# A gated MLP's down projection as seven half-size products, run in three blocks between the up tiles

## The chip, the core and the metric

The kernel runs on one core of a Trainium2 chip. The metric is the device time of one execution in microseconds (us). Five engines matter: TensorE (PE in the profile) does matmuls and transposes into PSUM, VectorE (DVE) and ScalarE (ACT) do elementwise work, GpSimd (POOL) does a few small powers, and SyncE (SP) issues the DMAs. Each engine works through its own list of instructions in order; semaphores hold an instruction until what it needs is done. A scheduling layer orders each list before the run and hands out the buffers of each pool.

## What is computed

The program is two encoder layers on 512 tokens of width 1024. The change touches the second half of each layer:

```
def conv_glu_ffn(x, w_up, conv_w, conv_b, w_down):       # x: 512 x 1024
    h = x @ w_up                                          # 512 x 5632
    hp = jnp.pad(h, ((0, 0), (1, 1), (0, 0)))
    h = hp[:, :-2] * conv_w[0] + hp[:, 1:-1] * conv_w[1] + hp[:, 2:] * conv_w[2] + conv_b
    a, b = jnp.split(h, 2, axis=-1)                       # 512 x 2816 each
    return (jax.nn.gelu(a) * b) @ w_down                  # 2816 x 1024
...
        ffn = conv_glu_ffn(x, w_up[i], conv_w[i], conv_b[i], w_down[i])
        ple = jax.nn.sigmoid(x @ w_ple_gate[i]) * (p[i] @ w_ple_proj[i])
        x = layer_norm(DEEPNORM_ALPHA * x + ffn + ple, ln2_g[i], ln2_b[i])
```

## The kernel before, in words

**Numbers in two parts.** Every matmul operand is split into a high part `hi` (ScalarE casts it, L96) and a rest `lo` (VectorE subtracts, L97). A product of two operands is three matmuls, `mm3` (L148 to L151): hi times hi, hi times lo, lo times hi, summed in PSUM. So each unit of matmul work comes as three instructions of 128x128 weights by 512 columns.

**Weights as a stream.** `Stream` (L99) brings all weights in the order of use, in 148 chunks of 128x1024 floats (512 KB) for each layer. `load` issues the DMA on SP into one of `N_RAW` = 3 raw buffers (L115); `prep` splits a chunk into one of `N_W` = 3 pairs of buffers in pool `wsplit`; `get` prepares two chunks ahead of the one handed out. Chunks listed in `RESIDENT` (L33) take their pair from pool `unit` instead (`up` in the code, 27 buffers of 4 KB in each partition), so that more of them can be ready. The last four of a layer are among these.

**The up projection.** For each of 22 tiles of 128 hidden channels (L677), two calls of `gemm_t` (L153; 24 matmuls each) give the two halves with channels on partitions and tokens on columns. ScalarE scales the middle tap (L683), VectorE adds the two neighbours (L684, L685), ScalarE applies gelu (L687), VectorE multiplies (L688), and the product is split (L690) into a buffer `gt` that stays until the down projection. All 22 pairs come first.

**The down projection.** It is one call of `proj_ln` (L217, called in L707) with 11 chunks for each of two column halves. For a chunk, `gn_part` (L163) does four token tiles with two blocks of 128 hidden channels each. This is 22 x 4 x 2 x 3 = 528 matmuls in a layer. The sums of a half stay in four PSUM banks for all 11 chunks. `half` then adds them to the residual tile `R` and takes the statistics (L224). In the second column half the last four chunks are worked token tile by token tile (`gemm_n_tok`, L181): so the layer norm of one tile (L235 to L239, with a power on GpSimd in L199) runs beside the matmuls of the next, and `done` of the tile before it is called. In the first layer, `done2` stores the tile to a scratch tensor and transposes it for the next layer (`to_xt`, L202); in the last it stores to the output. The transposes of the fourth tile wait in `pending` and run inside the next layer's first matmuls (L590).

Of the kernel before, what the change touches and what calls it, by code (L numbers as in the profile page):

```python
# [40 lines left out]
def _f(a):  # L41
    return a.bitcast(F32)


def trunk(tc, wpack, x_nat, x_tr, p_tr, rpb, decay, ln_par, conv, cos_t, sin_t, dist, xi_d, zd, mask, ident_d, out):
# [3 lines left out]
    with ExitStack() as es:  # L49
# [18 lines left out]
        def unit_r(s):  # L68
            return up.tile([P, 2, 512], F32R, tag="u", name=nm(s))
# [10 lines left out]
        def small(s, n):  # L80
            return sp.tile([P, n], F32, tag=f"s{n}", name=nm(s))
# [10 lines left out]
        nc.gpsimd.memset(mhalf, -0.5)  # L92


        def split(hi, lo, src):
            nc.scalar.copy(hi, src)  # L96
            nc.vector.tensor_sub(lo, src, _f(hi))  # L97

        class Stream:  # L99


            def __init__(self):
                self.seq = [(l, c) for l in range(DEPTH) for c in range(NCH)]
                self.nload = self.nprep = self.nget = 0
                self.raw, self.rdy = {}, {}

            def load(self, n, part=None):

                while self.nload < min(n, len(self.seq)):
                    l, c = self.seq[self.nload]  # L110
                    if self.nload not in self.raw:
                        self.raw[self.nload] = rp.tile([P, 1024], F32, tag="raw", name=f"raw_{l}_{c}")
                    r = self.raw[self.nload]
                    cs = slice(0, 1024) if part is None else slice(part * 512, (part + 1) * 512)
                    nc.sync.dma_start(r[:, cs], wpack[l, c][:, cs])  # L115
                    self.nload += part != 0
                    if part == 0:
                        return

            def prep(self, n, part=None):  # L120
                while self.nprep < min(n, len(self.seq)):
                    if part is None:
                        self.load(self.nprep + 1)
                    l, c = self.seq[self.nprep]
                    r = self.raw[self.nprep]
                    if self.nprep not in self.rdy:
                        pl, th, tl = (up, "u", "u") if (l, c) in RESIDENT else (wp, "hi", "lo")
                        hi = pl.tile([P, 1024], F32R, tag=th, name=f"hi_{l}_{c}")
                        lo = pl.tile([P, 1024], F32R, tag=tl, name=f"lo_{l}_{c}")
                        self.rdy[self.nprep] = (hi, lo)  # L130
                    hi, lo = self.rdy[self.nprep]
                    cs = slice(0, 1024) if part is None else slice(part * 512, (part + 1) * 512)
                    split(hi[:, cs], lo[:, cs], r[:, cs])
                    if part == 0:
                        return
                    del self.raw[self.nprep]
                    self.nprep += 1

            def get(self, ahead=2):
                self.prep(self.nget + 1 + ahead)  # L140
                self.load(self.nprep + N_RAW)
                w = self.rdy.pop(self.nget)
                self.nget += 1
                return w

        ws = Stream()

        def mm3(ps, lh, ll, rh, rl, start, stop):  # L148
            nc.tensor.matmul(ps, lh, rh, start=start, stop=False)  # L149
            nc.tensor.matmul(ps, lh, rl, start=False, stop=False)  # L150
            nc.tensor.matmul(ps, ll, rh, start=False, stop=stop)  # L151

        def gemm_t(xs, nk=8, wt=None, off=0):  # L153

# [15 lines left out]
        def gemm_n(lh, nchunk, pss, upto=None, post=None, ahead=lambda c: 2):  # L170
# [24 lines left out]
        def rstd_of(var, eps, n):  # L195
            v = small("ve", n)
            nc.vector.tensor_scalar_add(v, var, eps)
            r = small("rstd", n)
            nc.gpsimd.tensor_tensor(r, v, mhalf[:, :n], ALU.pow)  # L199
            return r  # L200
# [9 lines left out]
        def ln_consts(l, which):  # L210
# [3 lines left out]
            nc.sync.dma_start(b, ln_par[l, 2 * which + 1:2 * which + 2, :].to_broadcast([P, D]))  # L214
            return g, b

        def proj_ln(lh, nchunk, z, add, g, b, done, follow):  # L217

            st = [sp.tile([P, 2, 6], F32, tag="bn", name=nm("bn")) for _ in range(4)]

            def half(t, cb, ps):
                zz = z[t][:, cb * 512:(cb + 1) * 512]
                add(zz, ps)
                nc.vector.bn_stats(st[t][:, cb, :], zz)  # L224


            n1 = nchunk - 4
            deep = 4 + follow
            drain(gemm_n(lh, nchunk, [], post=lambda t, ps: half(t, 0, ps), ahead=lambda c: max(2, deep - 2 * (nchunk + n1 - 1 - c))))
            pss = []  # L230
            drain(gemm_n(lh, nchunk, pss, upto=n1, ahead=lambda c: max(2, deep - 2 * (n1 - 1 - c))))
            for t in gemm_n_tok(lh, nchunk, pss, nchunk - 4):
                half(t, 1, pss[t])
                mv = small("mv", 2)
                nc.vector.bn_aggr(mv, st[t])  # L235
                r = rstd_of(mv[:, 1:2], LN_EPS, 1)
                nc.vector.scalar_tensor_tensor(z[t], z[t], mv[:, 0:1], g, op0=ALU.subtract, op1=ALU.mult)
                for c in (slice(0, 512), slice(512, 1024)) if t == 3 else (slice(0, 1024),):
                    nc.vector.scalar_tensor_tensor(z[t][:, c], z[t][:, c], r, b[:, c], op0=ALU.mult, op1=ALU.add)  # L239
                if t:  # L240
                    done(t - 1)

# [57 lines left out]
        for l in range(DEPTH):  # L300
# [281 lines left out]
            if l == 0:  # L582
                drain(gemm_n(lhx, 4, [], post=lambda t, ps: v_tile(0, t, ps)))
                decay_logs()
            else:
                pss = []
                for t in gemm_n_tok(lhx, 4, pss, 0):
                    v_tile(0, t, pss[t])
                    if t == 1:
                        pending()  # L590
            drain(ret_inputs(0, True))

            plan = {}
# [79 lines left out]

            cw = bp.tile([P, 2 * NF, 4], F32, tag="cw", name=nm("cw"))
            nc.sync.dma_start(cw, conv[l])
            gt = []
            for i in range(NF):  # L677
# [11 lines left out]
                u = unit_r("gt")  # L689
                split(u[:, 0, :], u[:, 1, :], half[0])  # L690
                gt.append(u)


            g2, b2 = ln_consts(l, 1)
            last = l == DEPTH - 1
            if not last:
                xt = xp.tile([P, 8, 2, 512], F32R, tag="xt", name=nm("xt"))

            def done2(t, R=R, last=last, xt=xt):
                if last:  # L700
                    for c in (slice(0, 512), slice(512, 1024)):
                        nc.sync.dma_start(out[t * P:(t + 1) * P, c], R[t][:, c])
                else:
                    nc.sync.dma_start(scr[t * P:(t + 1) * P, :], R[t])
                    to_xt(xt, R[t], t)

            proj_ln(lambda k, s, t: gt[k][:, s, t * P:(t + 1) * P], 11, R, lambda zz, ps: nc.vector.tensor_add(zz, zz, ps), g2, b2, done2, 0 if last else 5)  # L707
            pending = lambda: done2(3)
        pending()


def _stat(w):
# [5 lines left out]
def _mov(w):  # L718

    K, N = w.shape  # L720
    return w.reshape(K // 256, 2, P, N // 512, 512).transpose(3, 0, 2, 1, 4).reshape(N // 512, K // 256, P, 1024)


def _pack(w_in, w_ba, w_bb, w_out, w_up, w_down, w_pg, w_pp):
# [20 lines left out]
    su = _stat(w_up)  # L745
    for i in range(NF):
        ch += [su[i], su[NF + i]]
    ch += list(_mov(w_down).reshape(-1, P, 1024))
    assert len(ch) == NCH
    return np.stack(ch)  # L750

# [64 lines left out]
```

## Time and profile before

| | us |
|---|---|
| median of 3 runs (1753.92 to 1754.45) | 1754.08 |
| the profiled execution | 1753.67 |
| its span from first to last instruction | 1751.4 |
| PE busy in the span | 1741.3 |
| VectorE busy | 1041.6 |
| ScalarE busy | 741.5 |
| up stage of the second layer, first to last matmul | 1384.2 to 1623.4 |
| down stage of the second layer, first to last matmul | 1623.6 to 1743.1 |

Two times of an instruction must be kept apart. A matmul's own duration is 389 ns in the rows, but the next one starts before it has ended; the distance from start to start is what a matmul costs the stream. "Busy" is the union of such times for PE. For the other engines durations don't overlap, and a duration is a cost. The idle time in a row is that of the engine just before the instruction, with what ended it.

### The profile page before, as it was taken

How to read it: one execution, taken by the hardware profiler on the slowest of the kernel's cores; microseconds unless marked ns; L12 is line 12 of the kernel's file. 1: busy time of each engine (PE TensorE's matmuls, PEld its weight loads, DVE VectorE, ACT ScalarE, POOL GpSimd, SP SyncE). 2: the span in 40 equal slices, each digit the busy share in tenths (PEclk: the TensorE clock that was granted, in tenths of full speed). 3: DMA queues.
4: the chain of work that ended last, by engine and by line, in shares of the span. 5: the costliest groups of instructions: out<-in, count | busy, mean ns of one | idle time of the engine just before them, and what ended most of it. 6: DMA issues, size and time to landing. Idle time of an engine off the chain costs nothing.

```text
span 1751.4 us, 20526 instructions
## 1 busy us (share of the span) xinstructions
PE 1741.3 (99%) x8169; PEld 1457.2 (83%) x8169; DVE 1041.6 (59%) x1577; ACT 741.5 (42%) x1100; POOL 35.1 (2%) x37
## 2 busy tenths in 40 slices
PE   9999999999999999999999999999999999999998
PEld 7888888888888888888888888888888888888886
DVE  6758766537546666633637687655475566666334
ACT  4535565544234444422234456655332344444220
POOL 0000000000100000000000000000001000000001
PEclk9999999999999999999999999999999999999999
DMA  6222222235122222233422121222351222222331
GB/s 236 87 73 84 69 85 92 89 136 181 48 97 96 97 96 97 96 109 109 162 76 87 61 97 61 95 86 85 133 180 49 93 100 96 97 96 97 108 121 60
DMA packets 52079, 175.78 MB, mean 100 GB/s; under 512 B 6032, under 2 KB 8592, under 8 KB 51984
## 3 DMA queue, kind: packets, MB, share of 16 engines
q1 hardware_dynamic: 51984, 174.48, 29.0%
q8 instruction: 64, 1.05, 0.2%
q14 instruction: 31, 0.25, 0.0%
HBM read 170.26 MB, written 4.19 MB: 100 GB/s over the span
## 4 chain that ended last, share of the span: by engine, by line
PE 96%; DVE 3%; DMA 0%; ACT 0%; issue 0%; POOLq 0%; SPq 0%; DVEq 0%; ACTq 0%
PE gt L150 17%; PE gt L149 17%; PE gt L151 17%; PE gn L150 12%; PE gn L151 12%; PE gn L149 12%; PE na L553 1%; PE pt L541 1%; PE o L151 1%; PE o L150 1%; PE o L149 1%; PE tr L206 1%; DVE lo L97 0%; PE ns L517 0%; PE ns L516 0%; PE ybt L436 0%
## 5 line engine op out<-in xcount | busy, mean ns | idle before, releaser
L97 DVE TENSOR_TENSOR lo<-raw,hi 128x1024 fp32r<-128x1024 f32 (+1 forms) x297 | 361.6, 1220 | 485.0 <-ACT hi L96 480.3
L96 ACT CAST hi<-raw 128x1024 fp32r<-128x1024 f32 (+1 forms) x297 | 310.6, 1049 | 491.8 <-PE gn L151 232.6
L149 PE MATMUL gt<-x1t,hi 128*128 128x512 f32 x704 | 273.9, 389 | 0.0
L150 PE MATMUL gt<-x1t,hi 128*128 128x512 f32 x704 | 273.9, 389 | 0.0
L151 PE MATMUL gt<-x1t,lo 128*128 128x512 f32 x704 | 273.9, 389 | 0.0
L149 PE MATMUL gt<-xt,hi 128*128 128x512 f32 x512 | 200.9, 392 | 0.0
L151 PE MATMUL gt<-xt,lo 128*128 128x512 f32 x512 | 199.6, 390 | 0.0
L150 PE MATMUL gt<-xt,hi 128*128 128x512 f32 x512 | 199.5, 390 | 0.0
L149 PEld LDWEIGHTS gt<-x1t,hi 128*128 128x128 f32 x704 | 132.2, 188 | 27.6
L151 PEld LDWEIGHTS gt<-x1t,lo 128*128 128x128 f32 x704 | 132.2, 188 | 27.3
L150 PEld LDWEIGHTS gt<-x1t,hi 128*128 128x128 f32 x704 | 132.2, 188 | 27.3
L149 PE MATMUL gn<-hi,gt 128*128 128x512 f32 x352 | 137.1, 389 | 0.0
L151 PE MATMUL gn<-hi,gt 128*128 128x512 f32 x352 | 136.9, 389 | 0.0
L150 PE MATMUL gn<-lo,gt 128*128 128x512 f32 x352 | 136.9, 389 | 0.0
L151 PEld LDWEIGHTS gt<-xt,lo 128*128 128x128 f32 x512 | 96.1, 188 | 20.3
L149 PEld LDWEIGHTS gt<-xt,hi 128*128 128x128 f32 x512 | 96.2, 188 | 19.1
L150 PEld LDWEIGHTS gt<-xt,hi 128*128 128x128 f32 x512 | 96.2, 188 | 19.0
L149 PE MATMUL gn<-hi,xt 128*128 128x512 f32 x256 | 100.3, 394 | 0.6 <-ACT hi L96 0.6
L150 PE MATMUL gn<-lo,xt 128*128 128x512 f32 x256 | 99.8, 390 | 0.0
L151 PE MATMUL gn<-hi,xt 128*128 128x512 f32 x256 | 99.7, 389 | 0.0
L96 ACT CAST gt<-ca 128x512 fp32r<-128x512 f32 x44 | 27.3, 621 | 122.0 <-DVE ca L688 122.0
L151 PEld LDWEIGHTS gn<-hi,gt 128*128 128x128 f32 x352 | 66.1, 188 | 13.8
(213 smaller groups left out, 2822.0 us busy)
## 6 DMA issues: line engine op xcount, KB each, us to landing
raw<-in_wpack SPq DMA_DIRECT2D x295, 512.0 KB, 3.2
xst<-in_x_tr SPq DMA_DIRECT2D x8, 256.0 KB, 6.2
xn<-in_x_nat SPq DMA_DIRECT2D x4, 512.0 KB, 6.2
lng<-in_ln_par SPq DMA_DIRECT2D x4, 512.0 KB, 5.0
lnb<-in_ln_par SPq DMA_DIRECT2D x4, 512.0 KB, 5.5
x_scr<-R SPq DMA_DIRECT2D x4, 512.0 KB, 2.6
xn<-x_scr SPq DMA_DIRECT2D x4, 512.0 KB, 6.5
out<-R SPq DMA_DIRECT2D x8, 256.0 KB, 2.0
```

The lines of the kernel that those rows point to most:

```text
L96: nc.scalar.copy(hi, src)
L97: nc.vector.tensor_sub(lo, src, _f(hi))
L149: nc.tensor.matmul(ps, lh, rh, start=start, stop=False)
L150: nc.tensor.matmul(ps, lh, rl, start=False, stop=False)
L151: nc.tensor.matmul(ps, ll, rh, start=False, stop=stop)
L206: nc.tensor.transpose(ps[:, k * P:(k + 1) * P], z[:, (4 * h + k) * P:(4 * h + k + 1) * P], ident)
L541: nc.tensor.transpose(ps[:, i * P:(i + 1) * P], S[:, g * 256 + bb * P:g * 256 + (bb + 1) * P], ident)
L553: nc.tensor.matmul(ov[kt], lv, pt[kt // 2][:, sp_, c], start=i == 0 and sp_ == 0, stop=i == 3 and sp_ == 1)
```

## The change

It does three things. The 22 up tiles of a layer are cut into three groups of 6, 8 and 8 (`SEGS` = 3, 4, 4 pairs), and after each group the part of the down projection that belongs to it is done, with the result added to `R`. That part is no longer eight block products but seven: tokens, hidden channels and output columns are each halved, and with sums and differences of blocks seven products of half size in each dimension are enough (the scheme of Strassen, in Winograd's form). In a pair of up tiles, `g1` and `g2` are the two halves of the hidden channels. Four sums of their token halves are made by VectorE in `s_parts` and split like any operand. The four quadrants of the weights are a, b, c and d. Their sums are not made on an engine: after a raw chunk has been split, a DMA issued by GpSimd adds the next quadrant to the chunk in place (`accum_op`), and the sum is split in turn. One chain goes a, a+b, a+b+d, a+b+c+d; another sum is b+d.

For `n` pairs a product is 2 x n x 3 matmuls. A product works in PSUM banks `u`, `v` (two each), or `w`, which sums its product over all three groups. After most products VectorE adds or subtracts the banks into `R` (`into`). The chunks of c take their pairs from pool `unit`; a raw chunk of a, and of b+d, is held there too. After the last group, the layer norms of the four tiles run beside the last two products and behind them. `done2` of tiles 0 and 1 is called after the last product, of tiles 2 and 3 in the next layer (or at the end).

```diff
-RESIDENT = {(1, c) for c in range(2)} | {(l, c) for l in range(DEPTH) for b in (68, 144) for c in range(b, b + 4)}
+SEGS = (3, 4, 4)
+LOOK = 3
+HELD = ("c",)
+DEEP = 4
+RESIDENT = {(1, c) for c in range(2)} | {(l, c) for l in range(DEPTH) for c in range(68, 72)}
...
+        def down_items(l, s):
...
+            for kind, src, plus in (("a", "a", None), ("c", "c", None), ("t1", None, "b"), ("t2", None, "d"),
+                                    ("d", "d", None), ("t3", "b", "d"), ("t4", None, "c")):
+                for j in range(2):
...
+                    it = Item(kind, at(src), pos["a", j][3], plus=at(plus), own=kind in ("a", "t3"), pool=up if kind in HELD else None)
+                    if kind in ("a", "t1", "t2", "t4"):
+                        if j in prev:
+                            prev[j].nxt = it
+                        prev[j] = it
...
+            def add(self, it):
+                l, c, o, w = it.plus
+                nc.gpsimd.dma_start(it.raw[:, :w], wpack[l, c][:, o:o + w], accum_op=ALU.add)
...
+                    if it.nxt is not None:
+                        it.nxt.raw = it.raw
+                        self.add(it.nxt)
...
+                def s_parts(p, g1, g2):
...
+                    nc.vector.tensor_sub(ta[:, H1], g2[:, H2], g1[:, H2])
+                    nc.vector.scalar_tensor_tensor(tb[:, H1], ta[:, H1], -1.0, g1[:, H1], **op)
+                    nc.vector.tensor_sub(tb[:, H2], g1[:, H1], g1[:, H2])
+                    nc.vector.scalar_tensor_tensor(ta[:, H2], tb[:, H1], -1.0, g2[:, H1], **op)
+                    sa[p], sb[p] = unit_r("sa"), unit_r("sb")
+                    split(sa[p][:, 0, :], sa[p][:, 1, :], ta)
+                    split(sb[p][:, 0, :], sb[p][:, 1, :], tb)
...
+                    split(a11[p][:, 0, :], a11[p][:, 1, :], g1[:, H1])
...
+                    split(k2[p][:, 0, :], k2[p][:, 1, :], g2)
...
+                def product(kind, ps, first):
...
+                    if kind == "t4":
+                        w = [ws.get(1), ws.get(2)]
+                        order = [(j, kk, i) for i in range(2) for j in range(2) for kk in range(2)]
+                    else:
+                        order = [(j, kk, i) for j in range(2) for i in range(2) for kk in range(2)]
...
+                        mm3(ps[i], lh(p, 0, i), lh(p, 1, i), hi[:, r], lo[:, r], first and p == 0, p == n - 1, not first)
...
+                product("a", u, True)
+                s_parts(*sums.pop())
+                for i in range(2):
+                    into(i, N1, u[i])
+                product("c", w, s == 0)
+                if fin:
+                    for i in range(2):
+                        into(i, N1, w[i])
+                        stats(i, 0)
+                product("t1", v, True)
+                for i in range(2):
+                    into(2 + i, N2, v[i], ALU.subtract)
+                product("t2", u, False)
+                for i in range(2):
+                    into(i, N2, u[i], ALU.subtract)
+                product("d", v, False)
+                for i in range(2):
+                    into(i, N2, v[i], ALU.subtract)
+                    stats(i, 1)
+                product("t3", u, False)
+                if fin:
+                    ln_tile(R[0], st[0], g2c, b2c, 1)
+                for i in range(2):
+                    into(2 + i, N2, u[i], ALU.subtract)
+                if fin:
+                    ln_tile(R[1], st[1], g2c, b2c, 1)
+                for i in range(2):
+                    stats(2 + i, 1)
+                product("t4", u, False)
+                if fin:
+                    done2(0)
+                    done2(1)
+                for i in range(2):
+                    into(2 + i, N1, u[i])
+                    stats(2 + i, 0)
+                    if fin:
+                        ln_tile(R[2 + i], st[2 + i], g2c, b2c, 2)
```

`ln_tile` is the layer norm of L235 to L239 as a function of its own; `fin` is true for the third group. In the built program, the lists of the stages before the up projection are the same as before but for a few places at the start of the second layer.

More of the change, by code (lines that the diff above doesn't have):

```diff
@@ L99, in trunk @@
         class Stream:
             def __init__(self):
-                self.seq = [(l, c) for l in range(DEPTH) for c in range(NCH)]
+                self.seq = []
+                for l in range(DEPTH):
+                    tile = 0
+                    plain = lambda c: self.seq.append(Item("w", (l, c, 0, 1024), 1024, pool=up if (l, c) in RESIDENT else None))
+                    for c in range(UP0):
+                        plain(c)
+                    for s, n in enumerate(SEGS):
+                        for c in range(UP0 + 2 * tile, UP0 + 2 * (tile + 2 * n)):
+                            plain(c)
+                        tile += 2 * n
+                        self.seq += down_items(l, s)
@@ L104, in __init__ @@
                 self.nload = self.nprep = self.nget = 0
-                self.raw, self.rdy = {}, {}
+            def add(self, it):
+                l, c, o, w = it.plus
+                nc.gpsimd.dma_start(it.raw[:, :w], wpack[l, c][:, o:o + w], accum_op=ALU.add)
             def load(self, n, part=None):
                 while self.nload < min(n, len(self.seq)):
[L110 to L115, printed above, removed]
+                    it = self.seq[self.nload]
+                    if it.src is None:
+                        self.nload += 1
+                        continue
+                    l, c, o, w = it.src
+                    if it.raw is None:
+                        if it.own:
+                            it.raw = up.tile([P, 1024], F32, tag="u", name=nm("raw" + it.kind))
+                        else:
+                            it.raw = rp.tile([P, 1024], F32, tag="raw", name=nm("raw"))
+                    cs = slice(0, w) if part is None else slice(part * 512, (part + 1) * 512)
+                    nc.sync.dma_start(it.raw[:, cs], wpack[l, c][:, o + cs.start:o + cs.stop])
+                    if it.plus is not None:
+                        self.add(it)
@@ L123, in prep @@
                         self.load(self.nprep + 1)
[L124 to L130, printed above, removed]
@@ L131, in prep @@
-                    hi, lo = self.rdy[self.nprep]
-                    cs = slice(0, 1024) if part is None else slice(part * 512, (part + 1) * 512)
-                    split(hi[:, cs], lo[:, cs], r[:, cs])
+                    it = self.seq[self.nprep]
+                    if it.hl is None:
+                        pl, th, tl = (up, "u", "u") if it.pool is not None else (wp, "hi", "lo")
+                        it.hl = (pl.tile([P, 1024], F32R, tag=th, name=nm("hi")), pl.tile([P, 1024], F32R, tag=tl, name=nm("lo")))
@@ L134, in prep, with get @@
+                    hi, lo = it.hl
+                    cs = slice(0, it.width) if part is None else slice(part * 512, (part + 1) * 512)
+                    split(hi[:, cs], lo[:, cs], it.raw[:, cs])
                     if part == 0:
                         return
-                    del self.raw[self.nprep]
+                    if it.nxt is not None:
+                        it.nxt.raw = it.raw
+                        self.add(it.nxt)
+                    it.raw = None
                     self.nprep += 1
[L139 to L142, printed above, removed]
+            def get(self, ahead=None):
+                if ahead is None:
+                    n, room = self.nget + 1, N_W - (self.seq[self.nget].pool is None)
+                    while n < min(len(self.seq), self.nget + 1 + DEEP):
+                        it = self.seq[n]
+                        if it.pool is None:
+                            if room == 0:
+                                break
+                            room -= 1
+                        elif it.kind == "w":
+                            break
+                        n += 1
+                    self.prep(n)
+                else:
+                    self.prep(self.nget + 1 + ahead)
+                self.load(self.nprep + LOOK)
+                it = self.seq[self.nget]
+                w, it.hl = it.hl, None
@@ L146, in trunk, with mm3 @@
         ws = Stream()
[L148 to L151, printed above, removed]
+        def mm3(ps, lh, ll, rh, rl, start, stop, more=False):
+            nc.tensor.matmul(ps, lh, rh, start=start, stop=False, skip_group_check=more)
+            nc.tensor.matmul(ps, lh, rl, start=False, stop=False, skip_group_check=more)
+            nc.tensor.matmul(ps, ll, rh, start=False, stop=stop, skip_group_check=more)
         def gemm_t(xs, nk=8, wt=None, off=0):
@@ L168, in gn_part, with gemm_n @@
                 mm3(ps, lh(k, 0, t), lh(k, 1, t), hi[:, r], lo[:, r], k == 0, k == 2 * nchunk - 1)
-        def gemm_n(lh, nchunk, pss, upto=None, post=None, ahead=lambda c: 2):
+        def gemm_n(lh, nchunk, pss, upto=None, post=None, ahead=lambda c: None):
             pss += [bank("gn") for _ in range(4)]
@@ L215, in ln_consts, with ln_tile @@
             return g, b
+        def ln_tile(z, st, g, b, parts):
+            mv = small("mv", 2)
+            nc.vector.bn_aggr(mv, st)
+            r = rstd_of(mv[:, 1:2], LN_EPS, 1)
+            nc.vector.scalar_tensor_tensor(z, z, mv[:, 0:1], g, op0=ALU.subtract, op1=ALU.mult)
+            for i in range(parts):
+                c = slice(i * D // parts, (i + 1) * D // parts)
+                nc.vector.scalar_tensor_tensor(z[:, c], z[:, c], r, b[:, c], op0=ALU.mult, op1=ALU.add)
         def proj_ln(lh, nchunk, z, add, g, b, done, follow):
@@ L233, in proj_ln @@
                 half(t, 1, pss[t])
[L234 to L239, printed above, removed]
+                ln_tile(z[t], st[t], g, b, 2 if t == 3 else 1)
                 if t:
@@ L675, in trunk, with up_tile @@
             nc.sync.dma_start(cw, conv[l])
-            gt = []
-            for i in range(NF):
+            last = l == DEPTH - 1
+            def up_tile(i):
                 half = []
@@ L688, in trunk @@
                 nc.vector.tensor_mul(half[0], half[0], half[1])
[L689 to L705, printed above, removed]
@@ L712, in _stat @@
+            pending = done2
+            if last:
+                pending(2)
+                pending(3)
 def _stat(w):
@@ L721, in _mov, with _blocks @@
     return w.reshape(K // 256, 2, P, N // 512, 512).transpose(3, 0, 2, 1, 4).reshape(N // 512, K // 256, P, 1024)
+def _blocks(w):
+    q = w.reshape(NF // 2, 2, P, 2, 512)
+    piece = lambda k, p0, p1: q[p0:p1, "ab".find(k) < 0 and 1 or 0, :, int(k in "bd")].transpose(1, 0, 2).reshape(P, -1)
+    ch, p0 = [], 0
+    for n in SEGS:
+        if n == 4:
+            ch += [piece(k, p0 + 2 * j, p0 + 2 * j + 2) for k in "acbd" for j in range(2)]
+        else:
+            ch += [piece(k, p0, p0 + 2) for k in "acbd"]
+            ch += [np.concatenate([piece(k, p0 + 2, p0 + 3) for k in kk], axis=1) for kk in ("ac", "bd")]
+        p0 += n
+    return ch
 def _pack(w_in, w_ba, w_bb, w_out, w_up, w_down, w_pg, w_pp):
@@ L747, in _pack @@
         ch += [su[i], su[NF + i]]
-    ch += list(_mov(w_down).reshape(-1, P, 1024))
+    ch += _blocks(w_down)
     assert len(ch) == NCH
```

95 lines of the change are left out of this document (88 added, 7 removed).

## The prediction

> **What bounds the kernel now.** I read the page's shares first, then the list of those who waited, then the groups of the down stage, then the timeline.
>
> ```profile
> PE 1741.3 (99%) x8169; PEld 1457.2 (83%) x8169; DVE 1041.6 (59%) x1577; ACT 741.5 (42%) x1100; POOL 35.1 (2%) x37
> ...
> PE gn L149 <- ACT hi L96: 0.6, 1, 0.6
> ...
> L149 PE MATMUL gt<-x1t,hi x352: 389/389/389, 513.9 to 752.6; 128*128 128x512 f32 x176
> ...
> 513.00:753.00 240.00, 240.00 (x1060) 198.79 (x1059) 146.74 (x177) 104.38 (x133) 0.00 (x0) 1.00 0.29 98
> 753.00:875.00 122.00, 122.00 (x550) 101.19 (x549) 52.62 (x60) 29.59 (x31) 4.33 (x3) 1.00 0.36 125
> 1622.00:1744.00 122.00, 121.44 (x536) 100.26 (x534) 45.06 (x51) 22.80 (x23) 4.34 (x3) 1.00 0.28 95
> ```
>
> PE is always busy, and after the start it waited for nobody longer than 0.6 us: its stream is the time. (The windows give PE, PEld, DVE, ACT and POOL busy, then the granted clock and the DMA share: up stage of layer 1, then the two down stages.) A matmul must not be priced by its 389 ns. The third line has 352 starts, three matmuls apart, from 513.9 to 752.6: 238.7/1053 = 0.2267 us a matmul. What keeps PE whole is slack elsewhere: VectorE is busy 61% in the up stage and about 40% in the down stage.
>
> These rows give the prices of the other engines, and the end of the kernel:
>
> ```profile
> L97 DVE TENSOR_TENSOR lo<-raw,hi 128x1024 fp32r<-128x1024 f32 x295 | 360.2, 1223 | 483.6 <-ACT hi L96 478.9 <-PE gn L151 3.9
> L97 DVE TENSOR_TENSOR gt<-ca,gt 128x512 fp32r<-128x512 f32 x44 | 30.5, 693 | 30.2 <-ACT gt L96 30.2
> L707 DVE TENSOR_TENSOR R<-R,gn 128x512 f32<-128x512 f32 x16 | 10.8, 684 | 20.2 <-PE gn L151 19.9
> L224 DVE BATCH_NORM_STATS2 bn<-R 128x6 f32<-128x512 f32 x16 | 10.7, 688 | 0.3
> L96 ACT CAST hi<-raw 128x1024 fp32r<-128x1024 f32 x295 | 309.4, 1051 | 490.2 <-PE gn L151 232.6 <-PE gt L150 125.1 <-issue 106.5
> ...
> 1743.05 0.39 PE L151 MATMUL gn<-hi,gt 128*128 128x512 f32 x1
> ...
> 1744.93 0.21 DVE L235 BATCH_NORM_AGGREGATE mv<-bn 128x2 f32<-128x12 f32 x1
> 1745.17 0.15 DVE L197 TENSOR_SCALAR ve<-mv 128x1 f32<-128x1 f32 x1
> 1745.24 1.28 DVE L237 SCALAR_TENSOR_TENSOR R<-R,mv,lng 128x1024 f32<-128x1024 f32 x1
> 1746.95 1.41 DVE L239 SCALAR_TENSOR_TENSOR R<-R,rstd,lnb 128x512 f32<-128x512 f32 x2 [0.43 <-POOL rstd L199]
> ...
> DMA to landing us min/median/max: 3.0/3.2/7.1
> ```
>
> A chunk's split is 1.05 us of ScalarE, then 1.22 of VectorE; a row of 512 elements is 0.69, one of 256 0.42 (or 0.48, `scalar_tensor_tensor`). VectorE ends 5.1 us after the stream's last step (1743.28 to 1748.36). The last line is a 512 KB raw chunk, from its issue.
>
> **What goes.** A product of n pairs is 2 x n x 3 matmuls, so a layer has 7 x 6 x 11 = 462 for 528. The built order of the changed kernel has 8027 matmuls for 8159; all 132 come from here, same shape. 132 x 0.2267 = **-29.9 us**, if the stream stays whole.
>
> **What VectorE gets.** A pair of up tiles is 96 matmuls, 21.8 us. VectorE had 4 x 1.22 + 8 x 0.75 + 4 x 0.69 = 13.6; a second split of 0.69 now becomes 0.42 + four sums 1.8 + two splits 1.4, together 16.5 (76%). A product block of four pairs is 168 matmuls, 38.1 us: 14 splits and 12 adds are 17.1 + 8.3 = 25.4. Hidden beside PE on the whole, as ScalarE's half of it is. The third block adds two adds, eight statistics and four layer norms (2.9 each): 25.4 + 1.4 + 5.5 + 11.7 = 44.0 against 38.1. That does not fit, so there I follow the built order of VectorE's list.
>
> **Waits inside the blocks.** Product t4 sums onto bank u, so the add that reads u after t3 must come first. VectorE's list has the splits of both t4 chunks ahead of that add, and the second split needs the buffer that t3's first chunk frees. From that moment PE has 12 matmuls left in t3 (2.72 us), the others 1.05 + 1.22 + 0.69 + 0.1 for gaps = 3.1: 0.35 late. With three pairs: 6 matmuls, 1.36, against 0.62 + 0.69 + 0.69 + 0.1 = 2.1: 0.75 late; there also t1's second chunk finds the sums of the last pair 0.5 late (from the last up matmul VectorE has 9.9 us of rows from 1.1 on, PE 10.9). 1.6 a layer, **+3.2**. Behind these adds in the list stand only the next chunks' splits, half a product early.
>
> **The third block.** Between d's end and the add that frees u, VectorE's list is: two adds, two statistics, a split, two aggregates, `ve`, the first layer-norm row, the other split, the second row, the add: 1.38 + 1.38 + 1.22 + 0.42 + 0.15 + 1.28 + 1.22 + 1.28 + 0.69 = 9.0, with 0.03 between rows 9.4. It can't begin early, since t3's second split fills the time until d ends. PE has only t3, 24 x 0.2267 = 5.4: PE stands for 3.9, in both layers **+7.8**. In layer 1 six transposes of tile 0 stand ahead of t4 and wait for the same rows.
>
> **The seam of the layers.** `done2(2)` is now in the next layer: its transposes are fixed in PE's list 19 matmuls into it. From t4's start VectorE has 19 rows up to tile 2's layer norm (an add, `ln_tile(R[1])`, statistics, four splits of transposes, a chunk's split, two more adds, the norm itself): 14.5, with gaps 15.0. PE has t4 5.4, ten transposes (eight took 1.03) 1.3, 19 matmuls 4.3: 11.0. **+3.9**; behind the waiting transposes stands the whole stream. The old kernel had tile 3 alone left here, and no wait.
>
> **The end.** From t4's start VectorE has `ln_tile(R[1])`, adds and statistics, and two layer norms: 14.1 in rows, 14.6 with gaps, less t4's 5.4 = 9.2 after the last matmul, for 5.1 now: **+4.1**. The output DMAs follow as before.
>
> **The adding DMAs.** There is no such row: GpSimd sent none. Let D be the time from an add's being free to go to its landing. It writes the 512 KB that a raw chunk does, so it is no less than 3.2; it also reads the buffer as a second stream, so at most twice the slowest row, 14.2. I take 5: 3.2, and 1.3 for a second stream at the 412 GB/s of the load at the start, and some for sending; DMA engines are only a third busy here. The cover: count from the last four up calls. They end at 21.8; a+b of chunk 0 is split then (its slot), by 24.1, and now the add of d may go. On ScalarE its split stands ahead of those of the last pair's sums `sa`, `sb`, which t1's second chunk needs at 32.6 (three pairs) or 36.0 (four). Going back over 1.05 + 1.22 + 0.69 and gaps, it must land by 30.1 or 32.9: cover 6.0 and 8.8. At D = 5 it costs **nothing**. On POOL's list the adds wait for each other's splits; b+d stands behind a+b+c+d there, with more cover. The weights are read twice over in all (8 quadrants for 4), in stages whose DMA share is 0.3. On SP's list the next up tiles' chunks stand behind b+d's loads, which wait for a `unit` buffer; they are due several products later.
>
> Sum: -29.9 + 3.2 + 7.8 + 3.9 + 4.1 = -10.9. Against the profiled execution's 1753.67 (span 1751.4 and 2.3 around it; 0.4 under the median) that is **1743**.
>
> **A rule against this change.** Three pauses of 3.9 us might cost more than themselves. The trace: PE's last matmul ends at 1743.4, and the windows show clock 1.00 to 1746, then
>
> ```profile
> 1746.00:1747.00 1.00, 0.00 (x0) 0.00 (x0) 0.56 (x2) 0.00 (x0) 0.92 (x1) 0.61 0.00 0
> ...
> 1.19 4.02 PE L248 MATMUL warm<-warm 128*128 128x512 bf16 x9 [1.19 <-DVE dl L282]
> ```
>
> The clock falls some 2.8 us after work stops, and at the start nine matmuls took 4.02, 0.45 each, twice the later pace. So each pause may cost up to 2 us more. The Trainium skill ("TensorE: Matmul & The Clock Gate", Part 1) says the clock halves after an idle window of about 3.4 us, which does not restart with the work; by that only some pauses of 3.9 would hold a whole window, and the sum would be 1743 or little more.
>
> **Rivals.**
> 1. Slow adds. Place: ScalarE's list before `sa`; price by steps at D = 10: three pairs 8.7 (k2 behind a+b 1.3, t1 4.3 more, t3 3.1), four pairs 3.0, third block 5.3: 17 a layer, +34, so **1777**. At D = 8 it is 3.2 + 1.5 a layer, +9.4, still 1752; from about 8.3 on the kernel is slower. For it: raw rows up to 7.1 and a second stream. Against: the median of 3.2. 0.28, and 0.07 for a D near 8.
> 2. VectorE's excess is hidden: rows overlap better than my chain, the third block's waits are some 1 us each. **1727**: 29.9 less 3.2. Against: the list's order is fixed. 0.13.
> 3. The clock falls in all three pauses: +6, **1749**. 0.12.
> 4. The matmuls are not fewer: excluded by the count.
>
> **How the numbers follow.** Forecast 1743 (0.40, some 1738 to 1747). This measurement tells 0.2% (3.5 us) from nothing. Faster: 0.40 + 0.13 + 0.10 of the third = 0.63; same: 0.07 + 0.02 = 0.09; slower: 0.28. From 1727 to 1775 leaves out a little of rival 2 below and half of rival 1 above (D beyond 10), 0.05 and 0.14.
>
> **What would show it.** Matmuls 132 fewer at 0.227 from start to start. Adds landing within 6 us. PE waiting for VectorE's `R` adds (t4) 0.3 to 0.8 in the first two blocks, 3.9 in the third, and 3.9 at tile 2's transposes; VectorE ending 9 us after the last matmul. Wrong if ScalarE's `hi` splits wait on DMAs for microseconds ahead of `sa`, or if the granted clock falls inside the kernel.

## The result, and the profile after

The changed kernel takes 1757.3 us (median; 1754.3 to 1760.23) where the kernel before takes 1753.88 (1753.42 to 1754.45) on the same chip. The ratio is 1.0019, 95% interval 1.0012 to 1.0026: slower by 0.2%, where 1743 was forecast. The profiled execution took 1758.16, its span 1756.4. The 132 matmuls went as counted (8037 records for 8169), so 29.9 us left PE's stream, and some 34 came in.

The page after the change: each engine's busy time, the DMA queues (packets, MB, share of 16 engines), the chain that ended last, and three DMA issues (KB each, median us to landing):

```profile
PE 1724.1 (98%) x8037; PEld 1436.5 (82%) x8037; DVE 1161.8 (66%) x1811; ACT 791.6 (45%) x1184; POOL 77.4 (4%) x85
...
q1 hardware_dynamic: 52560, 174.48, 29.1%
q0 software_dynamic: 6912, 23.07, 7.4%
...
PE 83%; issue 6%; DVE 5%; DMA 4%; ACT 1%; POOL 0%; SPq 0%; POOLq 0%; DVEq 0%; ACTq 0%
...
raw<-in_wpack SPq DMA_DIRECT2D x271, 512.0 KB, 3.3
rawa<-in_wpack POOLq DMA_DIRECT2D x30, 512.0 KB, 5.9
...
rawt<-in_wpack POOLq DMA_DIRECT2D x10, 512.0 KB, 7.9
```

The chain of the kernel before was:

```profile
PE 96%; DVE 3%; DMA 0%; ACT 0%; issue 0%; POOLq 0%; SPq 0%; DVEq 0%; ACTq 0%
```

PE is still busy 98%, but its part of the chain has gone from 96% to 83%, and DMA has 4% of it, where it had none. The two queues give a price. The loads (q1) hold the 16 engines for 0.291 x 1756.4 x 16 / 174.48 = 47 engine-us per MB, the adding DMAs (q0) for 90. A 512 KB load fills all sixteen for 1.54 us, an add for 2.95.

What PE waits for (in total, times, longest), after; before, after the start, the longest was 0.6:

```profile
PE u L233 <- DVE R L844: 7.4, 5, 2.3
PE v L233 <- ACT hi L101: 4.2, 1, 4.2
PE tr L290 <- DVE R L308: 2.8, 2, 1.5
PE u L234 <- DVE lo L103: 1.8, 4, 0.7
```

The first line is t4 waiting for its bank. The second and the fourth are waits for split weights, `hi` of ScalarE and `lo` of VectorE; nothing of the kind was forecast as a cost. By blocks, as PE time beyond 0.2267 us a matmul:

| stretch | layer 1 | layer 2 |
|---|---|---|
| three pairs | 6.7 | 8.6 |
| middle four pairs | 0.6 | 0.65 |
| third block (layer 1: with the seam) | 10.4 | 4.15 |
| behind the last matmul, over the 5.1 of before | | 2.7 |

About 8.5 of this is no wait but a slow clock behind a wait (the last section says when it comes). The largest piece is the third block of layer 1. In the windows (PE, PEld, DVE, ACT, POOL busy, granted clock, DMA share, GB/s) its first four products and then the pause are seen:

```profile
827.00:849.00 22.00, 22.00 (x98) 18.10 (x97) 17.01 (x24) 8.56 (x10) 5.29 (x6) 1.00 0.90 178
849.00:857.00 8.00, 3.80 (x16) 2.57 (x14) 1.59 (x2) 2.66 (x3) 0.00 (x0) 0.84 0.94 247
```

The DMA engines are not a third busy here but nine tenths, though 178 GB/s at a load's 47 engine-us per MB would be 0.52 of them. In the second window all compute engines starve together. ScalarE's and PE's lists of that moment (start, us, instruction, idle before):

```profile
844.02 1.06 ACT L101 CAST hi<-raw 128x1024 fp32r<-128x1024 f32 x1 [1.41 <-PE v L235]
854.34 1.99 ACT L101 CAST hi<-raw 128x1024 fp32r<-128x1024 f32 x2 [9.26 <-DMA raw<-in_wpack]
```

```profile
856.38 0.80 PE L233 MATMUL v<-hi,sa 128*128 128x512 f32 x1 [4.20 <-ACT hi L101]
857.83 0.79 PE L234 MATMUL v<-lo,sa 128*128 128x512 f32 x1 [0.65 <-DVE lo L103]
```

ScalarE stood 9.26 us for a plain load, a chunk of the next layer that took 8.8 us to land (issued at 845.51), and d's second chunk is behind it in the list. So an add need not be late itself; it makes the loads late. In the block of three pairs it is b+d that is late. GpSimd's list and ScalarE's split of it:

```profile
590.57 0.87 POOL L165 DMA_DIRECT2D rawa<-in_wpack  x1 [5.70 <-DVE lo L103]
591.12 1.22 POOL L165 DMA_DIRECT2D rawt<-in_wpack  x1
```

```profile
598.83 1.05 ACT L101 CAST hi<-rawt 128x1024 fp32r<-128x1024 f32 x1 [3.32 <-DMA rawt<-in_wpack]
```

b+d's add (`rawt`) stands behind a+b+c+d's, which stood 5.70 for a split of t2; then it took 7.6 us to land, the second one 11.0.

### The profile page after: what moved, and what is told of

It reads as the page before. It is cut to its first block, busy times and chain, and to the rows that moved or that the text cites. A ratio compares the mean times of both kernels' runs of the same rounds, so it can differ in the third digit from the quotient of the medians.

```text
span 1756.4 us, 20791 instructions
## 1 busy us (share of the span) xinstructions
PE 1724.1 (98%) x8037; PEld 1436.5 (82%) x8037; DVE 1161.8 (66%) x1811; ACT 791.6 (45%) x1184; POOL 77.4 (4%) x85
## 3 DMA queue, kind: packets, MB, share of 16 engines
q1 hardware_dynamic: 52560, 174.48, 29.1%
q0 software_dynamic: 6912, 23.07, 7.4%
## 4 chain that ended last, share of the span: by engine, by line
PE 83%; issue 6%; DVE 5%; DMA 4%; ACT 1%; POOL 0%; SPq 0%; POOLq 0%; DVEq 0%; ACTq 0%
PE gt L233 15%; PE gt L234 15%; PE gt L235 15%; PE gn L235 8%; PE gn L234 8%; PE gn L233 8%; DMA rawa<-in_wpack 2%; DVE lo L103 2%; PE u L233 2%; PE u L234 1%; PE u L235 1%; DMA rawt<-in_wpack 1%; ACT hi L101 1%; PE na L641 1%; PE pt L629 1%
## 5 line engine op out<-in xcount | busy, mean ns | idle before, releaser
L103 DVE TENSOR_TENSOR lo<-raw,hi 128x1024 fp32r<-128x1024 f32 (+1 forms) x277 | 334.7, 1210 | 344.2 <-ACT hi L101 343.4
L101 ACT CAST hi<-raw 128x1024 fp32r<-128x1024 f32 (+1 forms) x277 | 287.2, 1041 | 409.6 <-PE gt L234 118.4
L235 PE MATMUL gt<-x1t,lo 128*128 128x512 f32 x704 | 273.9, 389 | 0.0
L235 PE MATMUL gt<-xt,lo 128*128 128x512 f32 x512 | 199.6, 390 | 0.0
L235 PEld LDWEIGHTS gt<-x1t,lo 128*128 128x128 f32 x704 | 132.2, 188 | 27.5
L235 PEld LDWEIGHTS gt<-xt,lo 128*128 128x128 f32 x512 | 96.1, 188 | 20.3
L235 PE MATMUL gn<-hi,xt 128*128 128x512 f32 x256 | 99.7, 389 | 0.0
L103 DVE TENSOR_TENSOR lo<-rawa,hi 128x1024 fp32r<-128x1024 f32 (+1 forms) x48 | 54.1, 1131 | 42.0 <-ACT hi L101 42.0
L283 POOL TENSOR_TENSOR rstd<-ve,mhalf 128x2 f32<-128x2 f32 (+1 forms) x32 | 34.9, 1090 | 945.1 <-DVE ve L281 945.1
L101 ACT CAST hi<-rawa 128x1024 fp32r<-128x1024 f32 (+1 forms) x48 | 46.8, 979 | 64.1 <-DMA rawa<-in_wpack 34.2
L773 DVE SCALAR_TENSOR_TENSOR ca<-gt,cw,ca 128x511 f32<-128x511 f32 x88 | 65.5, 744 | 5.4 <-ACT ca L772 5.4
L772 ACT ACTIVATE ca<-gt,cw 128x512 f32<-128x512 f32 x88 | 68.2, 775 | 0.0
```

The source lines that it names most:

```text
L235: nc.tensor.matmul(ps, ll, rh, start=False, stop=stop, skip_group_check=more)
```

## The experiments

The theory: the adding DMAs cost twice the engine time of a plain transfer and crowd the DMA engines within the blocks, so splits come late. Its rivals: GpSimd's queue is slow whatever it carries; or it is VectorE's and ScalarE's order, with the adds only bystanders. The runs of before beside these had medians of 1754.01 (first four), 1754.09 (next four) and 1754.06 (last).

**Without the adds.** The chunks are split and used without the quadrant added, so the sums of the weights are not made.

```diff
-                nc.gpsimd.dma_start(it.raw[:, :w], wpack[l, c][:, o:o + w], accum_op=ALU.add)
+                return
```

> The changed kernel with its adding DMAs left out (so the sums of the weights' quadrants are not made; everything else is computed). Crowding theory (an add takes twice the DMA engines' time of a load, and in a block the 16 engines are full, so that sums and the loads beside them land late and PE stands): with no add in the way, PE's waits for splits (some 18 us with the slow clock behind them) go, and what is left is VectorE's rows at the third block, the seam and the end, 10 to 13 us; 1753.9 - 29.9 + 12 = about 1736. List theory (as in the prediction: the waits come from the fixed order and the amount of VectorE's work, not from DMAs): at most 3 us faster than the changed kernel's 1757, about 1754.

1737.05 us, ratio 0.9903 (0.9888 to 0.9918). Of PE's waits that the change brought, two lines are left:

```profile
PE u L233 <- DVE R L844: 4.6, 5, 2.3
PE tr L290 <- DVE R L308: 2.9, 2, 1.6
```

There is no wait for a split inside the blocks. The adds cost 20.3 us, two thirds of the 29.9 that the matmuls gave. Most of the other third is VectorE's order (the two lines above, and the end) with a slow clock behind one of its waits.

By blocks, PE's time beyond 0.2267 us a matmul falls by 5.7 and 7.5 in the blocks of three pairs and by 7.3 in layer 1's third block with the seam: 20.5 in these two profiles, for the 20.3 of the medians. The middle blocks lose no more with the adds than without (0.6), and neither does layer 2's third block (4.2 for 4.1), though each of them holds the same eight adds. A middle block of the changed kernel, with a DMA share of 0.79 (0.66 in 563 to 601 us, a block of three pairs), has PE busy without a break:

```profile
687.00:725.00 38.00, 38.00 (x169) 31.49 (x168) 28.16 (x38) 17.64 (x23) 7.04 (x8) 1.00 0.79 177
```

Its adds land in 5.5 to 10.3 us, as late as elsewhere. So the crowd alone cost nothing here; it cost where the late transfer had too little cover, that is, time between its landing and its use.

**The same DMAs, not adding.** They overwrite the buffer: same queue, same place in it, same bytes, and the sums are not made.

```diff
-                nc.gpsimd.dma_start(it.raw[:, :w], wpack[l, c][:, o:o + w], accum_op=ALU.add)
+                nc.gpsimd.dma_start(it.raw[:, :w], wpack[l, c][:, o:o + w])
```

> The same DMAs on the same queue in the same order, but they overwrite the buffer and don't add (so the products get a single quadrant for each sum). Crowding theory, with the adding as what doubles the engines' time: DMA share in the blocks falls from 1.0 to about 0.75, landings from 5.9 to about 4 us, time about 1742. If GpSimd's queue itself is what is slow, landings stay near 6 and the time near 1757. List theory: 1755 to 1757.

1739.04, ratio 0.9916 (0.9901 to 0.993). Its queue, and the two issues:

```profile
q0 software_dynamic: 6400, 23.07, 3.7%
...
rawa<-in_wpack POOLq DMA_DIRECT2D x30, 512.0 KB, 3.7
...
rawt<-in_wpack POOLq DMA_DIRECT2D x10, 512.0 KB, 4.8
```

The same 23.07 MB take 3.7% for 7.4%, and `rawa` lands in 3.7 for 5.9. So it is neither the queue nor the second reading of the weights, but the adding: 18.3 us of the 20.3.

**The next layer's first chunks not held back.** In the changed kernel they take pairs of their own from `unit`, and so their split stands ahead of d's.

```diff
-RESIDENT = {(1, c) for c in range(2)} | {(l, c) for l in range(DEPTH) for c in range(68, 72)}
+RESIDENT = {(l, c) for l in range(DEPTH) for c in range(68, 72)}
```

> The changed kernel, with the next layer's first two chunks no longer held in the unit pool, so that their splits don't stand ahead of d's on ScalarE in the first layer's third block. If d's second chunk was late only because ScalarE's list waited for a raw chunk of the next layer that landed late: the pause of 4.6 us, the 1.5 behind it and the slow clock's 1.5 go, about 1750. If the pause has another cause, as the list theory has it (VectorE's rows there), 1756 to 1758.

1754.78, ratio 1.0003 (0.9993 to 1.0013): between the two forecasts, 2.5 under the changed kernel, not the gain that the pause in d would have paid. That pause is gone, but in its place PE waits 3.2 before tile 0's transposes, and at the seam one matmul of the next layer 2.7 behind a layer norm. Most of it only moves. So the pause in d needed both: a load made late by the adds, and a place in ScalarE's list ahead of d's chunk.

**b+d ahead of the block.** Its load and its add are sent with a's loads, before the first product; the other adds stay.

```diff
+                    if kind == "a":
+                        firsts[j] = it
+                    if kind == "t3":
+                        firsts[j].early = it
...
+                    if it.early is not None and not it.early.loaded:
+                        e = it.early
...
+                        nc.sync.dma_start(e.raw[:, :w], wpack[l, c][:, o:o + w])
+                        self.add(e)
+                        e.loaded = True
```

> The changed kernel, with the load and the add of b+d issued together with the loads of a, before the block, so that they no longer stand behind a+b+c+d on GpSimd's list and no longer fall in the block's crowd. Crowding theory: the pauses ahead of t3 and t4 in the three-pair block (2.5 + 2.4 us, and the slow clock behind them 1.5 in layer 1 and 3.0 in layer 2) go in both layers, and DMA share in the blocks falls a little; about 1745. List theory: those pauses are VectorE's adds and stay; 1755 to 1757.

1738.78, ratio 0.9915 (0.99 to 0.9929): faster than both kernels, by more than expected. The same stretches of layer 1's third block, counted from its first matmul, and PE's waits:

```profile
822.00:844.00 22.00, 22.00 (x98) 18.21 (x97) 17.42 (x25) 10.04 (x12) 3.50 (x4) 1.00 0.73 139
844.00:852.00 8.00, 8.00 (x37) 6.62 (x36) 8.00 (x11) 3.65 (x5) 0.00 (x0) 1.00 0.70 229
```

```profile
PE u L246 <- DVE R L857: 4.6, 5, 2.3
PE tr L303 <- DVE R L321: 3.5, 2, 2.2
```

The DMA share is 0.73 for 0.90. The next layer's load at that place lands in 3.2 for 8.8, PE is busy without a break, and the waits for splits are gone as in the run without adds, though all the adds are made. What the adds still cost is 1.7 by the medians (1738.78 to 1737.05), with overlapping intervals. The adds' engine time has not fallen with the crowd: their queue takes 7.7% of the span of 1736.6, 93 engine-us per MB for 90.

**Loads sent five items ahead.** This is to tell whether b+d gained from its place in GpSimd's list or from leaving the crowd: it comes ahead of a+b+c+d in the list, but stays in the block. All other loads of the stream may go two items earlier too.

```diff
-LOOK = 3
+LOOK = 5
```

> The changed kernel with its loads sent five items ahead instead of three. That puts b+d's add ahead of a+b+c+d's in GpSimd's list, but still inside the block, with the same bytes in the same 38 us. Theory A, the crowd in the block (the DMA engines' time): the adds take 7 to 12 us still, and the time is 1752 to 1757. Theory B, b+d stood behind a+b+c+d's add, which waits for a split: PE's waits in t3 of the first block go (2.5 and 2.1, with some of the slow clock behind them), 1746 to 1750.

1747.07, ratio 0.9959 (0.9945 to 0.9974), in the range of theory B.

```profile
584.31 0.87 POOL L165 DMA_DIRECT2D rawa<-in_wpack  x1 [1.17 <-DVE lo L103]
585.16 0.92 POOL L165 DMA_DIRECT2D rawt<-in_wpack  x1
```

```profile
PE v L233 <- ACT hi L101: 3.3, 1, 3.3
```

b+d's first add goes 6 us sooner. It lands in 8.4, no faster, but in time; the blocks of three pairs give back 10.5 of their 15.3 us. The pause in d of layer 1 stays (3.3), with a share of 0.86 in the four products before it. So both theories hold, in different blocks: some 10 us (1757.3 to 1747.07) came with the earlier place in the list, and another 8 (1747.07 to 1738.78) with leaving the block. That the 10 are b+d's place alone is argued from the blocks in which they came back; the edit moves other loads too.

**VectorE's and ScalarE's order, with b+d ahead.** Three runs: the seam's edit again; the two adds that free bank u put ahead of tile 0's layer norm; and both.

```diff
                 product("t3", u, False)
-                if fin:
-                    ln_tile(R[0], st[0], g2c, b2c, 1)
                 for i in range(2):
                     into(2 + i, N2, u[i], ALU.subtract)
                 if fin:
+                    ln_tile(R[0], st[0], g2c, b2c, 1)
                     ln_tile(R[1], st[1], g2c, b2c, 1)
```

> This joins two edits: b+d's load and adding DMA ahead of the block (1738.8 alone), and the next layer's first two chunks no longer held back in the pairs' pool (1754.8 alone, no gain on the changed kernel). Theory A, the adding DMAs' crowd made the pause in d at the end of layer 1: with the crowd thinned that pause has gone already, so the second edit brings nothing, 1738 to 1740. Theory B, ScalarE's order (the next layer's split ahead of d's second chunk) has a price of its own: 1735 to 1737, with the seam's waits gone as well.

> Beside b+d going ahead of the block, in the third group the two adds that free bank u stand ahead of tile 0's layer norm in VectorE's list. Theory A, the order: PE's waits before t4 (2.2 and 2.3) shrink to some 0.5 each, and the slow clock behind the last one (1.7) goes: 1733 to 1735. Theory B, the amount of VectorE's work from d's end on: VectorE has no idle time from there to the transposes in layer 1 and to the last row in layer 2, so what PE gains before t4 it waits for at the transposes of tiles 0 to 2 and behind the last matmul: 1738 to 1739, the waits only in other places.

> All three edits: b+d ahead of the block, the next layer's first two chunks not held back, and the adds that free bank u ahead of tile 0's layer norm. If each of the last two has a gain of its own: 1731 to 1734. If both only move VectorE's work: 1737 to 1739.

The seam's edit: 1742.1 (0.9932, 0.9917 to 0.9946), worse than without it, which neither theory had: a matmul early in the next layer now waits 2.7 for a split behind layer-norm rows. The swap: 1738.0 (0.9909, 0.9894 to 0.9924); both: 1738.59 (0.9913, 0.9896 to 0.9929). The swap's null hides two opposite effects:

```profile
PE u L246 <- DVE R L857: 5.5, 6, 2.1
PE gn L247 <- DVE lo L103: 2.1, 1, 2.1
```

In layer 2 the wait before t4 went from 2.3 to 1.1, and no slow clock followed: about 3 us gained up to VectorE's last row. In layer 1 a chunk's split fell behind a norm (second line), with a slow clock behind it: as much lost.

**The swap in layer 2 alone.**

```diff
+                if fin and not last:
+                    ln_tile(R[0], st[0], g2c, b2c, 1)
                 for i in range(2):
                     into(2 + i, N2, u[i], ALU.subtract)
                 if fin:
+                    if last:
+                        ln_tile(R[0], st[0], g2c, b2c, 1)
```

> b+d ahead of the block, and the adds that free bank u ahead of tile 0's layer norm in the second layer alone. In the run with that order in both layers, layer 2's t4 stopped for 1.1 instead of 2.3 without a slow clock behind it, while in layer 1 a chunk's split fell behind a layer norm and cost about 3 at the seam. If these two are independent, layer 2's part stays alone: 1735 to 1736.5. If VectorE's work from d's end sets the end of the kernel whatever its order: 1738 to 1739.

1736.94, ratio 0.99 (0.9883 to 0.9916): the lowest of the versions that compute the whole, though its interval lies over those of b+d ahead (0.99 to 0.9929) and of the swap in both layers, so that this last step is not shown. It is under the 1738 of the second theory and a little over the first one's range, and its layer 2 shows the shorter wait (1.1, no slow clock), with the same 3.1 gained from the block's first matmul to VectorE's last row as in the swap of both layers.

## Why the prediction was wrong

**The step that failed: "At D = 5 it costs nothing".** The adding DMAs were priced at 0 and cost 20.3, by the profiles 13.2 in the blocks of three pairs and 7.3 in layer 1's third. They landed in 5.9 and 7.9 (the medians of `rawa` and `rawt`) and in up to 11.1, for the 5 assumed. Three parts of that step went wrong.
- "DMA engines are only a third busy here" and "in stages whose DMA share is 0.3". That share was the average of the old down stage. The change puts eight adds into a block of four pairs: 8 x 2.95 = 23.6 us of all sixteen engines in 38.1 us, 62% by themselves, and with the loads 0.79 in a middle block and 0.90 in the first four products of layer 1's third. Even without a row for an add, the text's own 1.3 us for a stream, taken twice for each add, gives 8 x 2.6 = 21 of the 38 us. This made the landings late, but where there was cover, as in the middle blocks, late landings cost nothing.
- "b+d stands behind a+b+c+d there, with more cover". In the blocks of three pairs it had less, and the text gave no number for it. The add ahead of it waits for a split in t2 and holds it on GpSimd's list to 591.12; what matters is not only when it is needed but when it may go.
- The price was put on the add alone. The loads on the other queue pay as well. The text looked at them for the next up tiles only ("they are due several products later"); at the end of layer 1 it is a chunk of the next layer, whose split stands ahead of d's in ScalarE's list. That plain 512 KB load took 8.8 us and stopped PE for the longest time of all.

The cover of `sa`, worked out at length, was nearly right: t1 lost 1.1 in one block of three pairs and 0.3 in the other.

**Rival 1, slow adds, is what came.** For D = 8 it had 1752, for D = 10 1777; 1757.3 lies between. But that number is in part luck, since its place was wrong: not ScalarE's list ahead of `sa`, but b+d in t3 and t4, and d.

**The matmuls: -29.9**, right, by count and by pace (24 in 5.44 us wherever nothing waits).

**Waits in the first two blocks: +3.2** forecast. With b+d ahead, t4 waits 0.77 in the blocks of three pairs and 0.38 in the middle ones, for 0.75 and 0.35; t1's 0.5 does not come. 2.3 in all.

**The third block 3.9 twice, the seam 3.9, the end +4.1**: each there, each too large. In the run with b+d ahead they are 2.2 and 2.3, 1.3, and 2.7 (VectorE ends 7.8 after the stream's last step for 5.1). The chain was priced at durations plus 0.03 between rows. In that run it reads, from d's end in layer 2 (left out are the layer norm's rows and the other split):

```profile
1710.08 1.28 DVE L857 TENSOR_TENSOR R<-R,v 128x512 f32<-128x512 f32 x2
1711.28 1.28 DVE L861 BATCH_NORM_STATS2 bn<-R 128x6 f32<-128x512 f32 x2
1712.47 1.21 DVE L103 TENSOR_TENSOR lo<-rawa,hi 128x1024 fp32r<-128x1024 f32 x1
...
1717.43 1.28 DVE L857 TENSOR_TENSOR R<-R,u 128x512 f32<-128x512 f32 x2
```

Two adds of 0.68 take 1.20 from start to start, 0.60 each. The chain to the end of the add that frees u is 1710.08 to 1718.11, 8.0 and not 9.4. The sections ahead of the prediction say that durations of engines other than PE don't overlap; in these rows VectorE's overlap by 0.08, and the chain came out too long mainly by that.

**The sum, mended.** -29.9 + 2.3 + 2.2 + 2.3 + 1.3 + 2.7, and 1.7 of slow clock, is -17.4; b+d ahead measured -15.2. The 2.2 that are left are in small steps of 0.1 to 0.5 around transposes and norms, and were not followed further. Rival 2 (1727, VectorE's excess hidden) is out: without any add the kernel takes 1737.

**Rival 3, the clock**, came as well, but not at its place: in the changed kernel it fell four times, behind t4 in both blocks of three pairs and in layer 2's third, after pauses of 2.4, and within the pause in d. In all it cost about 8.5 us there, and 1.7 with b+d ahead.

## What to carry to other kernels

Price DMA work in the stage where it runs: sum the engine time of the transfers that fall into one block and hold it against that block's length, because a share averaged over a longer stage hides a block that is nearly full. An adding DMA counts double there, and plain loads in the same window become late with it. Then look for the transfer with the least cover: the middle blocks were crowded too and lost nothing. Where several transfers share one issuing queue, send those that wait for no split first, ahead of the crowded block: here that alone turned +0.2% into -0.85%.

## What the runs showed of the hardware

**An adding DMA** takes 90 engine-us per MB, the same transfer on the same queue without adding 45, a load 47. The chunks `rawa` land in 5.9 (median, 512 KB) where the plain ones do in 3.7. In the crowd of the changed kernel an add took up to 11.1, and a plain load on SP's queue up to 12.9. The Trainium skill ("DMA: Bandwidth & Descriptors", Anatomy of one DMA) fits 2.0 us and the bytes at 436 KB per us for a DMA of GpSimd's, an estimate of 3.2 for 512 KB; the plain run agrees roughly (3.7), the adding one does not.

**VectorE's rows overlap.** An instruction that does not read the result of the one before it starts 0.08 us before that one's end; one that reads it starts 0.03 behind that end. Two rows of the kernel before, the statistics reading what the add wrote, show the second kind (0.72 from start to start, duration 0.69):

```profile
1743.48 0.69 DVE L707 TENSOR_TENSOR R<-R,gn 128x512 f32<-128x512 f32 x1 [0.68 <-PE gn L151]
1744.20 0.69 DVE L224 BATCH_NORM_STATS2 bn<-R 128x6 f32<-128x512 f32 x1
```

**The clock falls when PE stands for about half of a window of 3.41 us.** The trace has the times at which the granted clock goes from 1.0 to 0.5 and back. In each run they lie whole multiples of 3.4133 us apart: in the changed kernel it falls at 608.64, 854.40, 1482.45 and 1738.45, which is 0, 72, 256 and 331 such steps. If each run is cut into windows by these steps, then over all eleven profiles 17 windows between the clock's first rise and the last matmul began at full clock and had PE idle for 1.75 us or more, and the clock fell at the end of each. After some 5500 others, with 1.74 or less, it never fell. It then stays at 0.5 for one window or two, and a matmul costs 0.43 for 0.23: 1.5 to 2.9 us at a time behind the three such waits of t4 in the changed kernel.

So one and the same pause can cost more or less. Here is the wait before the last t4 in the changed kernel and in the one without adds; the last row of each is a stretch of 2 us in which the clock falls (the granted clock is the third number from its end):

```profile
1738.07 0.47 PE L233 MATMUL u<-hi,k 128*128 128x512 f32 x1 [2.28 <-DVE R L844]
1738.38 0.56 PE L234 MATMUL u<-lo,k 128*128 128x512 f32 x1
1738.73 0.63 PE L235 MATMUL u<-hi,k 128*128 128x512 f32 x1
1739.16 0.63 PE L233 MATMUL u<-hi,k 128*128 128x512 f32 x1
...
1738.00:1740.00 2.00, 1.93 (x5) 1.56 (x6) 2.00 (x4) 0.00 (x0) 1.27 (x1) 0.61 0.68 262
```

```profile
1717.60 0.47 PE L233 MATMUL u<-hi,k 128*128 128x512 f32 x1 [2.28 <-DVE R L844]
1717.91 0.39 PE L234 MATMUL u<-lo,k 128*128 128x512 f32 x1
1718.13 0.39 PE L235 MATMUL u<-hi,k 128*128 128x512 f32 x1
...
1718.00:1720.00 2.00, 2.00 (x9) 1.61 (x8) 2.00 (x5) 0.00 (x0) 1.45 (x1) 0.76 0.54 208
```

In the first the window ends 0.4 us behind the pause, and the steps are 0.43 almost at once. In the second it ends at 1719.06, 1.5 behind the pause: the steps are 0.23 until then, and eight of 0.43 follow. In the run in which only the next layer's chunks were not held back, a window ends within the same 2.28 us (at 1734.96, with 1.22 before it and 1.06 behind it), and the clock stays at 1.00. A wait of 1.1, as behind the swap, is under half a window wherever it falls. That the clock is judged by windows which run on by themselves agrees with the Trainium skill ("TensorE: Matmul & The Clock Gate", Part 1); that a whole idle window of about 3.4 us is needed does not: 1.75 were enough.
